# A two-layer attention, SSD and short-convolution kernel: step-size weights as 128 stationary columns, layer 1's rows high and low side by side, and a rule on which PSUM banks the unhurried work may take

## The chip, the cores and the metric

The kernel runs on one core of one Trainium2 chip. The metric is device time in microseconds (us). The kernel before took 1831.9 us, the median of three runs (1830.51 to 1834.58). A core has a matrix engine (PE, whose weight loads the profile lists as PEld), a vector engine (DVE), a scalar engine (ACT), a general engine (POOL) and SyncE (SP), which here issues most DMAs. Matmuls write to PSUM, which has eight banks of 128 partitions by 512 words of 4 bytes.

## The reference

The reference runs two layers over 256 latent tokens and 256 context tokens of width 2048. Layer 0 has neighbourhood attention and a bidirectional state-space scan (SSD), fed by one input projection. Two of its parts matter here. Step sizes, for each of 2 x 32 heads:

```python
dt = jax.nn.softplus(dt_raw + dt_bias)        # dt_raw = 64 columns of h @ w_in, 512 tokens
a = -jnp.exp(a_log)                           # the scan uses cumulated sums of dt * a
```

Layer 1 is a gated short convolution over the 256 latent tokens:

```python
p = h @ w_in                                  # 2048 x 8192
bg, cg, hv, g = jnp.split(p, 4, axis=-1)
y = bg * dw_conv(cg * hv, conv_w)             # 3 taps along the tokens
out = (jax.nn.silu(g) * y) @ w_out            # 2048 x 2048
```

A conditioning vector gives each layer a shift, a scale and a gate: matrix-vector products with `ada_w`, most of them done on DVE.

## The kernel before, in words

**Precision.** Every large product is done in three matmuls on numbers cut in two: a high part H (the value rounded to `fp32r`, a 32-bit type that the matrix engine takes at a faster rate) and a low part Lo (value minus H). A product of weights and rows is H·high + H·low + Lo·high. Each matmul loads its own 128-column stationary operand and streams its moving operand of 256 or 512 columns, one per token or per weight column.

**Weights.** `weight` queues loads of at most 512 KB (128 x 1024 words) from HBM, issued from SP into `raw` buffers. `split` makes H with a cast on ACT (L383) and Lo with a subtraction on DVE (L384). There are three pairs of H and Lo buffers (`NW = 3`), so that the cast for a load begins when the matmuls on the load three places earlier are done. `chunk` runs the matmuls of one load; `use` and `used` open and close it. All matmuls but the transposes have line L188, the helper `mm`; the transposes have L192.

**Order.** The order on every engine is fixed while the program is built. A planner (`Plan`) keeps a modelled clock for each engine. Work other than the matmuls of `chunk` is written as generators that yield what they wait for. After each few matmuls `pump` asks which generators may go on. Three lists hold them: `urgent` (drains of PSUM), `side` (attention heads and SSD groups) and `back` (the matrix-vector products, `gemv_gen`). A generator that wants a bank asks with `nb=1`. `banks(n)` takes n banks for a projection, and if too few are free it makes the drains go on first, wherever the matrix engine stands.

**Step sizes.** The 64 columns of `COL_DT` come in one load of 16 blocks (128 x 16 x 64). For each of 16 blocks of input channels, H·high, H·low and Lo·high go into the first 64 partitions of one bank, 512 tokens wide: 48 matmuls. `dt_gen` then computes softplus on a 64 x 512 layout with four `tmp` buffers, multiplies by `aneg`, and transposes both results in eight transposes.

**Layer 1, input projection.** For i = 0 to 3 and for each of the parts cg, hv, bg and gate, 512 columns of `sc_in` are projected: 8 loads of 2 blocks, and on each block four groups of 128 columns (`mm_ws` with n = 256). The weights are stationary, the 256 tokens move, and two groups share a bank, so that a part takes two banks. `cg_gen`, `hv_gen`, `bg_gen` and `gg_gen` drain them, in that order through `ordered`; `gg_gen` also makes the high and low halves (`y_0` to `y_15`) of the output projection's input. That projection runs four times over 8 loads, with two blocks and two token tiles on each load, 512 columns moving.

Of the kernel before, what the change touches and what calls it, by code (L numbers as in the profile page):

```python
# [8 lines left out]
F32 = mybir.dt.float32  # L9
# [6 lines left out]
KB = 16  # L16
# [125 lines left out]
def kernel(ctx: ExitStack, tc, x, cx, ada_w, ada_b, w_in, w_out, sc_in, sc_out, rpb, small, const,  # L142
                       strict, out):
# [233 lines left out]
    def split():  # L377
        k = pos["split"]
        raw, v = RAW.pop(k)
        nb, n = v.shape[1], v.shape[2]  # L380
        H = WH[k % NW][:, :nb * n].rearrange("p (b c) -> p b c", b=nb)
        Lo = WL[k % NW][:, :nb * n].rearrange("p (b c) -> p b c", b=nb)
        E(S.copy(H, v))  # L383
        E(V.tensor_tensor(out=Lo, in0=v, in1=H.bitcast(F32), op=ALU.subtract))  # L384
        HL[k] = (H, Lo)
        pos["split"] += 1
        give_raw(raw)
        issue()
# [104 lines left out]
    weight(w_in, 0, 16, COL_DT, 64)  # L493
# [117 lines left out]

    def chunk(kb0, kind, ps, first, last, lhs=None):

        H, Lo = use()
        nb = H.shape[1]
        for j in range(nb):
            kb = kb0 + j
            aH, aL = (hH[kb], hL[kb]) if lhs is None else lhs(kb)
            f, l = first and j == 0, last and j == nb - 1
            if kind == "act":  # L620
                mm_act(ps, aH, aL, H[:, j], Lo[:, j], f, l)
            else:
                mm_ws(ps, aH, aL, H[:, j], Lo[:, j], kind, f, l)
        used()
# [395 lines left out]
    aneg = st([128, 1], "aneg")  # L1020

    def dt_gen(ps):
        p64 = slice(0, 64)
        f, b = slice(0, 32), slice(32, 64)
        yield W_("ACT", ps)
        E(S.activation(aneg[p64], P_("alog")[p64], AF.Exp))
        E(V.tensor_scalar(out=aneg[p64], in0=aneg[p64], scalar1=-1.0, scalar2=None, op0=ALU.mult))
        tv, te, ts, ts2 = tmp(), tmp(), tmp(), tmp()
        v, e, s, s2 = tv[p64], te[p64], ts[p64], ts2[p64]
        E(S.activation(v, ps[p64], AF.Identity, bias=P_("dtb")[p64], scale=1.0))  # L1030
        give(free_b, ps)
        E(S.activation(e, v, AF.Abs))
        E(S.activation(e, e, AF.Exp, scale=-1.0))
        yield W_("DVE", te)
        E(V.tensor_scalar(out=s, in0=e, scalar1=2.0, scalar2=None, op0=ALU.add))
        E(V.reciprocal(s, s))  # L1036
        yield W_("DVE", ts)
# [3 lines left out]
        for k in (15, 13, 11, 9, 7, 5, 3):  # L1041
            yield W_("DVE", te)
            E(V.scalar_tensor_tensor(out=e, in0=e, scalar=1.0 / k, in1=s2, op0=ALU.add, op1=ALU.mult))
        yield W_("DVE", te)
        E(V.scalar_tensor_tensor(out=e, in0=e, scalar=1.0, in1=s, op0=ALU.add, op1=ALU.mult))
        E(V.tensor_scalar(out=v, in0=v, scalar1=0.0, scalar2=None, op0=ALU.max))
        E(V.scalar_tensor_tensor(out=v, in0=e, scalar=2.0, in1=v, op0=ALU.mult, op1=ALU.add))
        da = s2
        E(V.tensor_scalar(out=da, in0=v, scalar1=aneg[p64], scalar2=None, op0=ALU.mult))
        give(free_t, te, ts)  # L1050
        hm, ha = half(), half()
        dtm, dam = hm.rearrange("p (t c) -> p t c", t=4), ha.rearrange("p (t c) -> p t c", t=4)
        for src, dst in ((v, hm), (da, ha)):
            yield W_("PE", src, nb=1)
            pt = bank()
            for t in range(4):
                turn(pt[:, t * 64:(t + 1) * 64], src[:, t * 128:(t + 1) * 128])
            yield W_("DVE", pt)
            E(V.tensor_copy(dst, pt[:, :256]))
            give(free_b, pt)  # L1060
        give(free_t, tv, ts2)
# [3 lines left out]
        sS = half()  # L1065
# [35 lines left out]
        rw = tmp()  # L1101
# [295 lines left out]
    H, Lo = use()  # L1397
    for kb in range(KB):
        o = psD[:64, :]
        mm(o, H[:, kb], hH[kb], kb == 0, False)  # L1400
        mm(o, H[:, kb], hL[kb], False, False)
        mm(o, Lo[:, kb], hH[kb], False, kb == KB - 1)
        pump()
    used()
    spawn(urgent, dt_gen(psD), 4, 3)
# [85 lines left out]
    r1 = st([128, 2], "r1")  # L1491
    rb1 = []
# [17 lines left out]
    def norm_gen():  # L1510
# [13 lines left out]
        def low(kb):  # L1524
            E(V.scalar_tensor_tensor(out=hls[kb][:, 1], in0=late[kb], scalar=S1[:, kb:kb + 1], in1=hls[kb][:, 0].bitcast(F32),
                                     op0=ALU.add, op1=ALU.subtract))
            hH[kb], hL[kb] = hls[kb][:, 0], hls[kb][:, 1]
# [58 lines left out]

    def cg_gen(i, ps):
        for b in range(2):
            yield W_("ACT", ps[b])
            E(S.copy(flat(cg, b), ps[b]))  # L1590
            give(free_b, ps[b])

    def hv_gen(i, ps):
        for b in range(2):
            yield W_("DVE", ps[b], flat(cg, b))
            E(V.tensor_tensor(out=flat(u, b), in0=ps[b], in1=flat(cg, b), op=ALU.mult))
            give(free_b, ps[b])
        for b in range(4):
            ch = 4 * i + b
            yield W_("ACT", u[:, b, :])  # L1600
            E(S.mul(v[:, b, :], u[:, b, :], scw[:, 1, ch:ch + 1]))
            yield W_("DVE", v[:, b, :])
# [5 lines left out]
    def bg_gen(i, ps):  # L1608
        for b in range(2):
            yield W_("DVE", ps[b], flat(v, b))  # L1610
            E(V.tensor_tensor(out=flat(v, b), in0=ps[b], in1=flat(v, b), op=ALU.mult))
            give(free_b, ps[b])

    def gg_gen(i, ps):
        for b in range(2):
            yield W_("ACT", ps[b])
            th = tmp()
            E(S.activation(th, ps[b], AF.Tanh, scale=0.5))
            yield W_("DVE", th)
            E(V.scalar_tensor_tensor(out=th, in0=th, scalar=1.0, in1=ps[b], op0=ALU.add, op1=ALU.mult))  # L1620
            give(free_b, ps[b])
            yield W_("DVE", th, flat(v, b))
            E(V.tensor_tensor(out=flat(v, b), in0=flat(v, b), in1=th, op=ALU.mult))
            give(free_t, th)
            for j in range(2):
                kb = 4 * i + 2 * b + j
                yield W_("ACT", v[:, 2 * b + j, :])
                hl = st([128, 2, 256], f"hH{kb}", F32R, name=f"y2_{kb}")
                E(S.copy(hl[:, 0], v[:, 2 * b + j, :]))
                E(V.tensor_tensor(out=hl[:, 1], in0=v[:, 2 * b + j, :], in1=hl[:, 0].bitcast(F32), op=ALU.subtract))  # L1630
                y2[kb] = hl

    for i in range(4):
        for part, gen in ((1, cg_gen), (2, hv_gen), (0, bg_gen), (3, gg_gen)):
            ps = banks(2)
            for kb in range(0, KB, 2):
                force(lambda: hL[kb + 1] is not None)
                chunk(kb, 256, ps, kb == 0, kb == KB - 2)
            spawn(urgent, ordered(4 * i + (1, 2, 0, 3).index(part), gen(i, ps)), 1 if part == 3 else 0)
# [30 lines left out]
_INS = ['x', 'cx', 'ada_w', 'ada_b', 'w_in', 'w_out', 'sc_in', 'sc_out', 'rpb', 'small', 'const', 'strict']  # L1670
# [48 lines left out]
```

## Time and profile before

| what | value |
|---|---|
| median of three runs | 1831.9 us |
| the profiled execution's own time | 1833.06 us |
| its span, first to last instruction | 1831.3 us |
| instructions | 28234 |
| bytes moved by DMA | 376.95 MB, 206 GB/s over the span |
| TensorE clock granted over the span | 0.997 of full |

The span ends 1.8 us short of the execution's own time, which is what lies around the program. The stages in the trace: up to 100 us the loads set the pace; layer 0 with its output projection runs to about 1357 us; a normalisation stands between the layers; layer 1's input projection runs from 1365 to about 1738 us and its output projection to the end.

In the profile a matmul's duration (0.28 us for 256 columns, 0.39 us for 512) is its time from issue to its modelled end. Consecutive matmuls overlap, so what a matmul costs is the distance between two starts, which the view in order of time shows.

### The profile page before, as it was taken

Reading aid. Unit: us, or ns where it says so; the run is one execution under the profiler, and the core shown is the slowest. Engines: PE = TensorE matmul, PEld = TensorE weight load, DVE = VectorE, ACT = ScalarE, POOL = GpSimd, SP = SyncE. Lnnn points to the kernel's source line nnn. Section 1 sums busy time; section 2 is a strip of 40 time slices with the busy share of each in tenths; the row PEclk is TensorE's granted clock in tenths of the full one; section 3 lists DMA queues with packets and bytes.
Section 4 is the critical chain, followed back from the end, with each engine's and each line's share of the span. In section 5 each row is a group of like instructions: output and inputs, shape, how many; then the busy total and the mean of one; then the engine's idle time right before and its main releaser. Section 6 shows DMA issues by size and latency. Waiting matters only on the chain.

```text
span 1831.3 us, 28234 instructions
## 1 busy us (share of the span) xinstructions
PE 1798.7 (98%) x11003; PEld 1546.3 (84%) x11003; DVE 1236.5 (68%) x1943; ACT 762.6 (42%) x1303; POOL 29.5 (2%) x27
## 2 busy tenths in 40 slices
PE   6999999999999999999999999999999999999998
PEld 4677977888888888888878898888879999999987
DVE  5566785877565887575876678756667666555555
ACT  5322533445232445242444345544444344444442
POOL 0000000001000001000001000000000000000000
PEclk9999999999999999999999999999999999999999
DMA  9997644575656575655564557777867777656564
GB/s 327 334 299 250 213 130 122 160 226 175 185 166 190 160 230 179 191 184 187 161 202 144 185 168 221 219 223 261 271 220 230 228 235 239 209 183 181 183 209 155
DMA packets 249062, 376.95 MB, mean 206 GB/s; under 512 B 32624, under 2 KB 103888, under 8 KB 248928
## 3 DMA queue, kind: packets, MB, share of 16 engines
q1 hardware_dynamic: 239632, 366.57, 64.2%
q10 hardware_dynamic: 9296, 8.57, 1.4%
q8 instruction: 86, 1.41, 0.3%
q14 instruction: 48, 0.39, 0.1%
HBM read 368.63 MB, written 7.77 MB: 206 GB/s over the span
## 4 chain that ended last, share of the span: by engine, by line
PE 77%; issue 10%; DVE 4%; DMA 3%; ACT 2%; SPq 0%; POOL 0%; ACTq 0%; POOLq 0%; DVEq 0%
PE bank L188 75%; PE bank L192 2%; DMA tmp<-dram_csr 2%; DVE wL L384 1%; ACT wH L383 1%; DMA raw<-in_w_in 1%; DVE tmp L1122 1%; DVE tmp L1292 0%; DVE tmp L1303 0%; DMA raw<-in_w_out 0%; DVE tmp L1036 0%; ACT tmp L885 0%; DVE acc L752 0%; ACT tmp L1288 0%; DVE tmp L1306 0%
## 5 line engine op out<-in xcount | busy, mean ns | idle before, releaser
L384 DVE TENSOR_TENSOR wL<-raw,wH 128x1024 fp32r<-128x1024 f32 (+1 forms) x440 | 533.9, 1217 | 352.0 <-ACT wH L383 350.7
L383 ACT CAST wH<-raw 128x1024 fp32r<-128x1024 f32 (+1 forms) x440 | 458.9, 1045 | 736.9 <-PE bank L188 648.8
L188 PE MATMUL bank<-h,wH 128*128 128x256 f32 x2048 | 371.5, 284 | 1.3 <-ACT h L1534 1.1
L188 PE MATMUL bank<-hH,wH 128*128 128x256 f32 (+2 forms) x1040 | 352.8, 339 | 0.9 <-ACT wH L383 0.9
L188 PE MATMUL bank<-hL,wH 128*128 128x256 f32 (+2 forms) x1040 | 338.1, 325 | 0.0
L188 PE MATMUL bank<-hH,wL 128*128 128x256 f32 (+2 forms) x1040 | 337.3, 324 | 0.6 <-DVE wL L384 0.5
L188 PEld LDWEIGHTS bank<-h,wH 128*128 128x128 f32 x2048 | 320.9, 193 | 2.7 <-ACT h L1534 1.3
L188 PE MATMUL bank<-h,wL 128*128 128x256 f32 x1024 | 290.6, 284 | 0.0
L188 PE MATMUL bank<-wH,hH 128*128 128x512 f32 x640 | 258.4, 404 | 3.9 <-ACT hH L695 2.6
L188 PE MATMUL bank<-wL,hH 128*128 128x512 f32 x640 | 251.1, 393 | 0.0
L188 PE MATMUL bank<-wH,hL 128*128 128x512 f32 x640 | 250.2, 392 | 0.1
L752 DVE SCALAR_TENSOR_TENSOR acc<-raw,csil,acc 128x512 f32<-128x512 f32 x256 | 191.9, 750 | 71.7 <-DMA raw<-in_ada_w 66.7
L188 PEld LDWEIGHTS bank<-hH,wH 128*128 128x128 f32 (+1 forms) x1040 | 195.7, 188 | 25.3 <-issue 7.3
L188 PEld LDWEIGHTS bank<-hH,wL 128*128 128x128 f32 (+1 forms) x1040 | 196.1, 189 | 19.9 <-DVE wL L384 1.7
L188 PEld LDWEIGHTS bank<-hL,wH 128*128 128x128 f32 (+1 forms) x1040 | 196.0, 188 | 19.9 <-issue 4.3
L188 PEld LDWEIGHTS bank<-h,wL 128*128 128x128 f32 x1024 | 197.3, 193 | 0.1
L188 PE MATMUL bank<-wH,mix 128*128 128x512 f32 x512 | 163.5, 396 | 0.0
L188 PEld LDWEIGHTS bank<-wH,hH 128*128 128x128 f32 x640 | 120.5, 188 | 36.3 <-issue 7.1
L188 PEld LDWEIGHTS bank<-wH,hL 128*128 128x128 f32 x640 | 120.5, 188 | 26.3 <-DVE hL L701 0.6
L188 PEld LDWEIGHTS bank<-wL,hH 128*128 128x128 f32 x640 | 120.8, 189 | 24.1 <-DVE wL L397 0.3
L188 PEld LDWEIGHTS bank<-wH,mix 128*128 128x128 f32 x512 | 96.1, 188 | 21.3 <-issue 1.4
L188 PE MATMUL bank<-wL,mix 128*128 128x512 f32 x256 | 99.8, 390 | 0.0
(233 smaller groups left out, 1613.2 us busy)
## 6 DMA issues: line engine op xcount, KB each, us to landing
raw<-in_w_in SPq DMA_DIRECT2D x211, 512.0 KB
raw<-in_ada_w SPq DMA_DIRECT2D x162, 512.0 KB
raw<-in_sc_in SPq DMA_DIRECT2D x128, 512.0 KB
raw<-in_w_out SPq DMA_DIRECT2D x64, 512.0 KB
raw<-in_sc_out SPq DMA_DIRECT2D x32, 512.0 KB
tmp<-dram_csr SPq DMA_DIRECT2D x32, 256.0 KB
PT<-in_ada_w SPq DMA_DIRECT2D x14, 512.0 KB
xtm<-in_ada_w SPq DMA_DIRECT2D x9, 512.0 KB
```

What stands on the lines that cost most here:

```text
L188: E(T.matmul(o, l, r, start=start, stop=stop, skip_group_check=True))
L192: E(T.transpose(o, i, ident if k == 128 else ident[:k, :k]))
L383: E(S.copy(H, v))
L384: E(V.tensor_tensor(out=Lo, in0=v, in1=H.bitcast(F32), op=ALU.subtract))
L752: E(V.scalar_tensor_tensor(out=acc, in0=v[:, j], scalar=csil[:, 2 * k + j:2 * k + j + 1], in1=acc, op0=ALU.mult, op1=ALU.add))
L1122: E(V.scalar_tensor_tensor(out=do, in0=di, scalar=cwh[:, 32 * k + ch:32 * k + ch + 1], in1=do, op0=ALU.mult, op1=ALU.add))
```

## The change

Three edits.

1. **Step sizes.** The load is cut in two of 8 blocks (128 x 8 x 64). `split` writes H into columns 0 to 63 and Lo into columns 64 to 127 of one stationary block. Two matmuls for each block of input channels (with the high and the low rows moving) fill all 128 partitions of a bank: 32 matmuls. `dt_gen` copies the bank to one `tmp`, turns it in four 128 x 128 transposes, adds the halves, and does softplus on a 128 x 256 layout. Bias and decay now come as rows (`rows`, one DMA broadcast to all partitions).
2. **Layer 1.** The rows' high and low parts already lie side by side in `hls` (128 x 2 x 256). `mm_both` moves them as one operand of 512 columns over H, and then the high 256 alone over Lo. Each group of 128 columns has its own bank, so that a part takes four banks; its high and low sums lie in the two halves and are added by `both` (a copy on ACT, an addition on DVE). The four drains now go by 256 columns in four steps instead of 512 in two.
3. **Banks.** In `may`, work from `back` that asks for a bank is held until the free bank that was left first has been left for 3000 ns by the planner's clock.

```diff
+        if hor < 2000 and nb and sorted(plan.last[b.tensor.name] for b in free_b)[nb - 1] + 3000 > now:
+            return False
...
+        if n == 64:
+            W = WH[k % NW].rearrange("p (b c) -> p b c", b=nb)
+            E(S.copy(W[:, :, :64], v))
+            E(V.tensor_tensor(out=W[:, :, 64:], in0=v, in1=W[:, :, :64].bitcast(F32), op=ALU.subtract))
...
-    weight(w_in, 0, 16, COL_DT, 64)
+    for r0 in (0, 1024):
+        weight(w_in, r0, 8, COL_DT, 64)
...
+    def mm_both(ps, act, H, Lo, first, last):
+        for b, o in enumerate(ps):
+            bb = slice(b * 128, (b + 1) * 128)
+            mm(o, H[:, bb], act, first, False)
+            mm(o[:, :256], Lo[:, bb], act[:, :256], False, last)
+            if b % 2:
+                pump()
...
-        E(S.activation(v, ps[p64], AF.Identity, bias=P_("dtb")[p64], scale=1.0))
...
+        E(DMA.dma_start(rw[:, :128], rows[0].partition_broadcast(128)))
+        yield W_("ACT", ps)
+        E(S.copy(tt, ps))
         give(free_b, ps)
+        yield W_("PE", tt, nb=1)
+        pt = bank()
+        for t in range(4):
+            turn(pt[:, t * 128:(t + 1) * 128], tt[:, t * 128:(t + 1) * 128])
...
-    for kb in range(KB):
-        o = psD[:64, :]
-        mm(o, H[:, kb], hH[kb], kb == 0, False)
-        mm(o, H[:, kb], hL[kb], False, False)
-        mm(o, Lo[:, kb], hH[kb], False, kb == KB - 1)
...
+        for kb in range(8 * k, 8 * k + 8):
+            mm(psD, W[:, kb - 8 * k], hH[kb], kb == 0, False)
+            mm(psD, W[:, kb - 8 * k], hL[kb], False, kb == KB - 1)
...
+    def both(p, o=None):
+        yield W_("ACT", p)
+        o = half() if o is None else o
+        E(S.copy(o, p[:, 256:]))
+        yield W_("DVE", o)
+        E(V.tensor_tensor(out=o, in0=p[:, :256], in1=o, op=ALU.add))
+        give(free_b, p)
+        return o
...
     def gg_gen(i, ps):
-        for b in range(2):
...
+        for b in range(4):
+            kb = 4 * i + b
+            gg = yield from both(ps[b])
+            yield W_("ACT", gg)
+            th = half()
+            E(S.activation(th, gg, AF.Tanh, scale=0.5))
+            yield W_("DVE", v[:, b, :])
+            E(V.tensor_tensor(out=v[:, b, :], in0=gg, in1=v[:, b, :], op=ALU.mult))
...
-            ps = banks(2)
+            ps = banks(4)
...
-                chunk(kb, 256, ps, kb == 0, kb == KB - 2)
+                chunk(kb, "both", ps, kb == 0, kb == KB - 2, lambda i: (h1[i], None))
```

How the order moves on the matrix engine in layer 1: here it begins with the second group of the first block before. `h_0` is the rows' first block with its high and low halves, `wH` and `wL` the cut weights; "x2" is the matmul with the high and then with the low half.

```order
L188 MATMUL bank_86<-h_0_10398,wH_99 128x256 x2
L188 MATMUL bank_86<-h_0_10398,wL_102 128x256
L188 MATMUL bank_90<-h_0_10398,wH_99 128x256 x2
L188 MATMUL bank_90<-h_0_10398,wL_102 128x256
L188 MATMUL bank_90<-h_0_10398,wH_99 128x256 x2
L188 MATMUL bank_90<-h_0_10398,wL_102 128x256
```

The same place after the change:

```order
L188 MATMUL bank_85<-h_0_10352,wL_100 128x256
L188 MATMUL bank_90<-h_0_10352,wH_97 128x512
L188 MATMUL bank_90<-h_0_10352,wL_100 128x256
L188 MATMUL bank_89<-h_0_10352,wH_97 128x512
L188 MATMUL bank_89<-h_0_10352,wL_100 128x256
L188 MATMUL bank_84<-h_0_10352,wH_97 128x512
L188 MATMUL bank_84<-h_0_10352,wL_100 128x256
```

Three matmuls of 256 columns on one group became one of 512 and one of 256, and four banks are written in turn instead of two.

The second place is DVE at the seam between layer 1's two projections, before the change. `wL` rows are the weight subtractions of `split`; `y_12` to `y_15` are the last four blocks of the output projection's input, written here by `gg_gen` for i = 3. The first subtraction shown belongs to the output projection's load 3, counted from 0, and the second to load 4.

```order
L384 TENSOR_TENSOR wL_101<-raw_93,wH_98 128x1024
L1630 TENSOR_TENSOR y_12_14149<-v,y_12_14149 128x256
L1630 TENSOR_TENSOR y_13_14152<-v,y_13_14152 128x256
L1620 SCALAR_TENSOR_TENSOR tmp_66<-tmp_66,bank_91 128x512
L1623 TENSOR_TENSOR v<-v,tmp_66 128x512
L384 TENSOR_TENSOR wL_102<-raw_94,wH_99 128x1024
L1630 TENSOR_TENSOR y_14_14182<-v,y_14_14182 128x256
L1630 TENSOR_TENSOR y_15_14185<-v,y_15_14185 128x256
```

After the change, the end of the same drain, with the subtractions of loads 7, 8 and 9:

```order
L396 TENSOR_TENSOR wL_100<-raw_93,wH_97 128x1024
L1668 TENSOR_TENSOR y_14_13332<-v,y_14_13332 128x256
L1622 TENSOR_TENSOR half_77<-bank_87,half_77 128x256
L396 TENSOR_TENSOR wL_101<-raw_94,wH_98 128x1024
L1661 TENSOR_TENSOR v<-half_77,v 128x256
L1663 SCALAR_TENSOR_TENSOR v<-half_83,v 128x256
L396 TENSOR_TENSOR wL_102<-raw_95,wH_99 128x1024
L1668 TENSOR_TENSOR y_15_13370<-v,y_15_13370 128x256
```

`y_15` moved from behind the subtraction of load 4 to behind that of load 9; between two of the four blocks there are now two weight subtractions.

The third place is the matrix engine in the step-size product. Before, three rows for one block of input channels:

```order
L188 MATMUL bank_91<-hH_328,wH_98 64x512
L188 MATMUL bank_91<-hL_332,wH_98 64x512
L188 MATMUL bank_91<-hH_328,wL_101 64x512
L192 MATMUL bank_87<-const,tmp_66 128x128 x4
L188 MATMUL bank_91<-hH_519,wH_98 64x512
```

After it, two rows for a block:

```order
L188 MATMUL bank_90<-hH_321,wH_98 128x512
L188 MATMUL bank_90<-hL_325,wH_98 128x512
L192 MATMUL bank_87<-const,tmp_66 128x128 x4
L188 MATMUL bank_90<-hH_328,wH_98 128x512
L188 MATMUL bank_90<-hL_332,wH_98 128x512
```

The matmul with the separate `wL` is gone, and the other two write 128 partitions instead of 64; the transposes between them are another generator's.

More of the change, by code (lines that the diff above doesn't have):

```diff
@@ L142 @@
 def kernel(ctx: ExitStack, tc, x, cx, ada_w, ada_b, w_in, w_out, sc_in, sc_out, rpb, small, const,
-                       strict, out):
+                       strict, rows, out):
     nc = tc.nc
@@ L1491 @@
     r1 = st([128, 2], "r1")
+    h1 = {}
     rb1 = []
@@ L1585, in ordered @@
         seq[0] += 1
+    def both(p, o=None):
[6 more added lines that the diff above has]
+        return o
     def cg_gen(i, ps):
-        for b in range(2):
-            yield W_("ACT", ps[b])
-            E(S.copy(flat(cg, b), ps[b]))
-            give(free_b, ps[b])
+        for b in range(4):
+            yield from both(ps[b], cg[:, b, :])
     def hv_gen(i, ps):
[L1594 to L1597, printed above, removed]
         for b in range(4):
             ch = 4 * i + b
+            yield from both(ps[b], u[:, b, :])
+            yield W_("DVE", u[:, b, :])
+            E(V.tensor_tensor(out=u[:, b, :], in0=u[:, b, :], in1=cg[:, b, :], op=ALU.mult))
             yield W_("ACT", u[:, b, :])
             E(S.mul(v[:, b, :], u[:, b, :], scw[:, 1, ch:ch + 1]))
+        for b in range(4):
+            ch = 4 * i + b
             yield W_("DVE", v[:, b, :])
@@ L1608, in bg_gen @@
     def bg_gen(i, ps):
[L1609 to L1612, printed above, removed]
-    def gg_gen(i, ps):
[L1615 to L1618, printed above, removed]
-            yield W_("DVE", th)
[L1620 to L1631, printed above, removed]
+        for b in range(4):
+            bg = yield from both(ps[b])
+            yield W_("DVE", bg, v[:, b, :])
+            E(V.tensor_tensor(out=v[:, b, :], in0=bg, in1=v[:, b, :], op=ALU.mult))
+            give(free_h, bg)
@@ new lines, in gg_gen @@
+    def gg_gen(i, ps):
+        for b in range(4):
+            kb = 4 * i + b
[5 more added lines that the diff above has]
+            E(V.tensor_tensor(out=v[:, b, :], in0=gg, in1=v[:, b, :], op=ALU.mult))
+            yield W_("DVE", th)
+            E(V.scalar_tensor_tensor(out=v[:, b, :], in0=th, scalar=1.0, in1=v[:, b, :], op0=ALU.add, op1=ALU.mult))
+            give(free_h, gg, th)
+            yield W_("ACT", v[:, b, :])
+            hl = st([128, 2, 256], f"hH{kb}", F32R, name=f"y2_{kb}")
+            E(S.copy(hl[:, 0], v[:, b, :]))
+            E(V.tensor_tensor(out=hl[:, 1], in0=v[:, b, :], in1=hl[:, 0].bitcast(F32), op=ALU.subtract))
+            y2[kb] = hl
@@ L1667 @@
     force(lambda: not urgent, (urgent,))
-_INS = ['x', 'cx', 'ada_w', 'ada_b', 'w_in', 'w_out', 'sc_in', 'sc_out', 'rpb', 'small', 'const', 'strict']
+_INS = ['x', 'cx', 'ada_w', 'ada_b', 'w_in', 'w_out', 'sc_in', 'sc_out', 'rpb', 'small', 'const', 'strict', 'rows']
 def kernel(**inputs):
@@ L1706 @@
         'w_out': f('na_ssd_w_out')[0], 'sc_in': f('sc_w_in')[0], 'sc_out': f('sc_w_out')[0], 'rpb': f('na_rpb')[0],
-        'small': small, 'const': const, 'strict': strict}
+        'small': small, 'const': const, 'strict': strict,
+        'rows': np.concatenate([f('ssd_dt_bias')[0].reshape(1, 64), f('ssd_a_log')[0].reshape(1, 64)], axis=1)}
     nc = bacc.Bacc("TRN2", target_bir_lowering=False, num_devices=1)
```

77 lines of the change are left out of this document (42 added, 35 removed).

## The prediction

> **What bounds the kernel now.** The first part of the page, the busy time of each engine, comes first.
>
> ```profile
> PE 1798.7 (98%) x11003; PEld 1546.3 (84%) x11003; DVE 1236.5 (68%) x1943; ACT 762.6 (42%) x1303; POOL 29.5 (2%) x27
> ```
>
> The matrix engine is busy all the time, with DVE at two thirds. That share is a mean, so the next view is the busy time by stage (stretch, its length, then PE, PEld, DVE, ACT and POOL with counts, the granted clock, DMA share, GB/s).
>
> ```profile
> 100.00:1350.00 1250.00, 1247.82 (x6905) 1039.67 (x6904) 889.35 (x1463) 517.52 (x976) 25.88 (x16) 1.00 0.64 197
> 1350.00:1400.00 50.00, 46.16 (x324) 43.27 (x323) 35.84 (x60) 27.42 (x45) 0.70 (x1) 0.93 0.58 192
> ...
> 1737.00:1831.00 94.00, 88.77 (x395) 73.04 (x393) 51.66 (x55) 33.87 (x36) 0.00 (x0) 1.00 0.58 182
> ```
>
> Layer 0 leaves PE idle for 2.2 of 1250 us, the seam between the layers for 3.8. Then the chain that ended last, in order of time: start, length, what.
>
> ```profile
> 1364.99 19.62 PE bank L188 x144
> 1384.62 1.21 DVE wL L384
> 1385.83 0.33 DVE yi L1532
> 1386.16 0.41 DVE h L1525
> ```
> ```profile
> 1386.61 438.50 PE bank L188 x3320
> ```
>
> From 1386.6 us to 1825 us the chain is one row of matmuls: no wait stands in it. In layer 1 a matmul's start-to-start distance is time itself, so I read those distances from the view in order of time (start, length, instruction).
>
> ```profile
> 1499.87 0.28 PE L188 MATMUL bank<-h,wL 128*128 128x256 f32 x1
> ...
> 1501.67 0.28 PE L188 MATMUL bank<-h,wL 128*128 128x256 f32 x1
> ```
> ```profile
> 195.69 0.39 PE L188 MATMUL bank<-wH,hL 128*128 128x512 f32 x1
> ...
> 200.00 0.39 PE L188 MATMUL bank<-wL,hH 128*128 128x512 f32 x1
> ```
>
> Between the first two rows lie five rounds of three matmuls: 15 in 1.80 us, 120.0 ns for 256 columns. Between the other two lie 19 steps in 4.31 us: 226.8 ns for 512. Twice the columns do not cost twice the time. A line through both has 0.417 ns for a column and 13.2 ns for a matmul whatever its length. On that 13.2 ns the forecast rests.
>
> **Layer 1's input projection.** It has 16 parts x 16 blocks x 4 groups = 1024 groups. Before, a group takes three matmuls of 256: 360.0 ns. After, it takes one of 512 and one of 256: 346.8 ns. The columns streamed stay 768; one matmul with its weight load goes. 1024 x 13.2 ns = **13.5 us**, all on the path, since nothing else ends there.
>
> The trace has no stream that alternates 512 and 256, so the pair has to be bounded. On the good side, the weight loads fill the all-256 stream:
>
> ```profile
> 1500.00:1550.00 50.00, 50.00 (x419) 50.00 (x418) 33.97 (x41) 19.42 (x21) 0.00 (x0) 1.00 0.73 239
> ```
>
> PEld is busy 50.00 of 50 us there. If loads are what holds 256 columns at 120 ns, a 256 beside a 512 could come down to half of 226.8, which is 113.4: a pair of 340 and a gain of 20.3 us. On the bad side, the longest distance for 512 columns that repeats is in the step-size product:
>
> ```profile
> 231.15 0.40 PE L188 MATMUL bank<-hH,wH 128*64 128x512 f32 x1
> ...
> 235.78 0.40 PE L188 MATMUL bank<-hH,wL 128*64 128x512 f32 x1
> ```
>
> 20 steps in 4.63 us: 231.5 ns. With that and a 256 as much worse (124), the pair is 355 and the gain 5 us. I take 346.8, because the two rows it is made of are long streams of just these operations, and because 64 stationary columns cost no less than 128: the surcharge goes with the instruction, not with the load's width.
>
> The Trainium skill speaks against this gain. "TensorE: Matmul & The Clock Gate", section "Back-to-back issue gap", gives N/2.4 + 2.5 ns between matmuls. That would be 109 and 216 ns, a fixed part of 2.5 ns, and here a gain of 1024 x 2.5 = 2.6 us (an estimate from that page). The trace agrees on the slope (0.417) and not on the fixed part (13.2).
>
> **What the drains add.** Each bank now costs a copy on ACT and an addition on DVE, and the products run by 256. The nearest rows, by group (count, then busy us and mean ns, idle before):
>
> ```profile
> L384 DVE TENSOR_TENSOR wL<-raw,wH 128x1024 fp32r<-128x1024 f32 x121 | 147.6, 1224 | 125.2 <-ACT wH L383 125.2
> L383 ACT CAST wH<-raw 128x1024 fp32r<-128x1024 f32 x120 | 125.7, 1047 | 192.9 <-PE bank L188 183.0 <-DVE acc L742 3.8 <-issue 1.5
> ...
> L1596 DVE TENSOR_TENSOR u<-bank,cg 128x512 f32<-128x512 f32 x8 | 5.1, 682 | 0.0
> ...
> L1590 ACT COPY cg<-bank 128x512 f32<-128x512 f32 x8 | 4.3, 586 | 0.0
> L1623 DVE TENSOR_TENSOR v<-v,tmp 128x512 f32<-128x512 f32 x6 | 4.2, 692 | 0.2
> ```
> ```profile
> 1390.00:1737.00 347.00, 347.00 (x2904) 346.00 (x2904) 210.75 (x238) 142.99 (x162) 0.00 (x0) 1.00 0.68 213
> ```
> ```profile
> 291.05 0.42 DVE L1011 TENSOR_TENSOR half<-bank,gt 128x256 f32<-128x256 f32 x1 [0.57 <-PE bank L188]
> ```
>
> For each i, eight DVE operations at 0.69 us (5.5 us) become 32 at 0.42 (13.4 us), and four on ACT at 0.59 become 16 copies and four tanh at about 0.4 (2.4 to 8 us). Over the window that is some 30 us more on DVE (to about 72% busy) and 20 on ACT (to about 49%). Both had been idle waiting for the matrix engine's progress (125 and 183 us, the releasers above), so I cost it at nothing. If that cover were gone, the price is the slower rival below.
>
> The banks: all eight are now used, four filling and four draining. The order shows the gate's drain as four steps with two weight subtractions in each. A load lasts 8 x 346.8 ns = 2.77 us, so that a step is about 5.6 us and the last bank comes free about 3 x 5.6 + 2 = 19 us into the next part, which takes 22.2 us. So nothing waits there.
>
> At the seam to the output projection something does. `y_15` now stands on DVE behind the weight subtraction of load 9, whose cast begins only when load 6 is done; and load 7 is what needs `y_15`.
>
> ```profile
> 1749.36 1.05 ACT L383 CAST wH<-raw 128x1024 fp32r<-128x1024 f32 x1 [1.69 <-PE bank L188]
> ```
> ```profile
> 1742.16 1.23 DVE L384 TENSOR_TENSOR wL<-raw,wH 128x1024 fp32r<-128x1024 f32 x1 [0.32 <-ACT wH L383]
> 1743.30 0.75 DVE L1630 TENSOR_TENSOR y<-v,y 128x256 fp32r<-128x256 f32 x2
> ...
> 1750.43 1.22 DVE L384 TENSOR_TENSOR wL<-raw,wH 128x1024 fp32r<-128x1024 f32 x1 [1.51 <-ACT wH L383]
> ```
>
> After load 6: cast to subtraction 1.07, subtraction to `y` 1.14, `y` 0.4, together 2.7 us. The matrix engine has 8 matmuls before it needs that low part, 1.8 us. **Cost 0.9 us.**
>
> At the start of layer 1 the chain quoted above shows the first part held by the normalisation at 1384.62 (wL, then yi, then h). The order is the same there after the change, so a faster matrix engine partly waits: of its first part's 64 x 13.2 ns = 0.85 us I give back 0.5.
>
> **Step sizes.** 48 matmuls become 32, all 512 columns long; a 64-column stationary block costs 231.5 ns, no less than a full one: 16 x 231.5 = **3.7 us**. The transposes go from eight of 64 columns to four of 128, which cancels. Two loads of half the size move the same 256-byte pieces past the same SP queue; they need two `raw` buffers and two weight slots for a while. The chain behind it gets shorter:
>
> ```profile
> 244.82 3.35 DVE L1036 RECIPROCAL tmp<-tmp 64x512 f32<-64x512 f32 x1
> ```
>
> At half the width this should be near 1.7 us, and the steps behind it shrink likewise. Layer 0's matrix engine hardly idles, so I count nothing for it. The `strict` load now waits on SP for the decay product; its generator asks for it only when the planner has that product done, so that the weight loads behind it are not held for long.
>
> **The bank rule.** It concerns the matrix-vector products alone.
>
> ```profile
> L188 PE MATMUL bank<-acc,const 128*32 128x128 f32 x24 | 1.3, 285 | 0.0
> ```
>
> Nothing waited before them (idle 0.0), so there is nothing to save before; it guards the fuller banks after. Its result can come later: the order has 12 of the 16 products ahead of layer 1 now, not 13, and the last well before the output projection. Cost nothing.
>
> **Reordering.** The edit at 230 us shifts what is interleaved in all of layer 0. By PE's idle time there is only 2.2 us to win; stalls shorter than a matmul's modelled length do not show, so I allow 4 us either way, middle zero.
>
> **Sum.** 1833.06 - 13.5 - 3.7 + 0.9 + 0.5 = 1817.3 us in the terms of the profiled execution. The median of the runs stands 1.2 us below that execution, so the forecast is **1816.1 us**, 0.9% faster.
>
> **Rivals.**
> *Loads were the limit* (the 340 ns pair): 6.8 us more, 1809.3. For it speaks PEld at 50.00 of 50; against it, that 512 columns, where loads have twice the time, carry the same surcharge. Chance 0.09.
> *The surcharge does not go with the instruction.* If a short matmul between long ones pays for the one that was dropped, a group stays at 360 ns and only the step sizes are left: 1816.1 + 13.5 = 1829.6. Nothing in the trace has this mix, so it cannot be excluded; the straight line is against it. Chance 0.05.
> *Most of it goes with the group.* If only about 2.5 of the 13.2 ns belong to a matmul and the rest is paid once for a group of 128 columns, layer 1 gains 2.6 us: 1827.0. The straight line is against this too, since the 512-column stream changes its group as often as the other and pays the same. Chance 0.03. The rule of the Trainium skill above ("TensorE: Matmul & The Clock Gate") amounts to this.
> *The drains hold the banks*, which ends slower. Let s be a step of the gate's drain. A part begins late by 3s + 2 - 22.2 us, three times; the seam by about 4s - 20.9 (at s = 5.45, eight loads of the output projection's 2.72 us in four steps, that is the 0.9 above). At s = 5.6 the first is nothing; at s = 7.9 both together are 21 us, which eats the gain and 3.7 us more, and that is the point from which it decides. With a third weight subtraction in each step (s = 8.4) they come to 15 + 12.7 = 27.7 us, 26.8 over the forecast: 1842.9. Against it, DVE has 28% of the stage free. Chance 0.05.
> *The change does not do what it says*: the order shows the 512 and 256 pairs and the 32 matmuls, so this is left only for the bank rule, at no price.
>
> **How the numbers follow.** The forecast has 0.78, with its own range of 1811 to 1823: the 4 us of reordering, and the pair within about 2 ns. The range for 8 in 10 goes down to 1808 for the first rival and up to 1824.5 for the pair at 355 ns. A measurement can tell 0.2%, 3.7 us, from no change: faster 0.90 (the forecast, the loads and the group), the same 0.05, slower 0.05.
>
> **What would show it.** In order of time, starts in layer 1 should go 227, 120, 227, 120 ns; a sum of 340 or 360 names the rival. The step-size product should last about 7.4 us instead of 11. The output projection's load 7 should begin with a wait of 1 us on DVE `y`, and no other row but PE should stand in the chain from 1390 us on. DVE or ACT drains in the chain in layer 1, or a wait at the first matmul of a part, would be the slower rival. A layer 0 that ends more than 4 us off (its output projection now ends at 1357 us, and 3.7 us earlier is expected) would make the prediction wrong for a reason not worked out here.

## The result, and the profile after

| | before | after |
|---|---|---|
| median of six runs each | 1832.62 us (1830.51 to 1834.58) | 1822.1 us (1820.64 to 1825.36) |
| ratio, 95% interval | | 0.994 (0.993 to 0.9951) |
| the profiled execution's own time | 1833.06 us | 1820.64 us |
| its span | 1831.3 us | 1818.9 us |

The change is faster by 10.5 us, 0.6%; 15.8 us (0.9%) had been forecast. The forecast of 1816.1 us lies 6.0 us under the median, and its range holds it. The profiled execution of the changed kernel is the fastest of its six, so that the two traces stand 12.4 us apart, and it is those 12.4 us that the views can place.

The page's first part, the busy time of each engine, of the changed kernel:

```profile
PE 1785.2 (98%) x9959; PEld 1488.2 (82%) x9959; DVE 1259.2 (69%) x2039; ACT 777.4 (43%) x1369; POOL 28.5 (2%) x27
```

There are 1044 matmuls fewer, and the share of PE is still 98%: the program got shorter with its bound, and the bound is the same. DVE and ACT did more (1236.5 and 762.6 us before), in less time. The busy time by stage of the changed kernel (columns as in the prediction):

```profile
100.00:1350.00 1250.00, 1248.66 (x6895) 1043.44 (x6894) 877.71 (x1450) 518.99 (x978) 24.90 (x16) 1.00 0.64 195
1350.00:1400.00 50.00, 45.08 (x243) 37.93 (x243) 36.83 (x63) 27.22 (x46) 0.70 (x1) 0.97 0.58 188
1400.00:1720.00 320.00, 320.00 (x1850) 277.41 (x1849) 233.48 (x327) 149.80 (x210) 0.00 (x0) 1.00 0.73 228
1720.00:1819.00 99.00, 92.72 (x410) 75.52 (x408) 55.15 (x64) 36.14 (x43) 0.00 (x0) 0.99 0.57 180
```

From 1400 to 1720 us PE is busy 320.00 of 320 us: no wait for a drain shows (one shorter than the overlap of two matmuls would not). DVE is at 73% there (233.48 of 320) and ACT at 47%. PEld, which was full before (50.00 of 50), is at 87%. The chain that ended last in the changed kernel (start, length, what):

```profile
1381.66 360.68 PE bank L188 x2055
1742.33 1.35 issue
1743.68 1.06 ACT wH L395
1745.10 0.81 issue
1746.38 66.37 PE bank L188 x289
```

Before, one row of matmuls ran from 1386.61 to 1825 us. Now it breaks once, at 1742 to 1746 us, where a cast on ACT stands in it: the seam to the output projection.

Each stage's length, from the first matmul of one stage to that of the next, in the views in order of time of both kernels (us). For the changed kernel the first two of these matmuls are:

```profile
1360.56 0.79 PE L188 MATMUL bank<-h,wH 128*128 128x512 f32 x1 [1.57 <-DVE h L1553]
...
1724.27 0.39 PE L188 MATMUL bank<-wH,y 128*128 128x512 f32 x1
```

| stage | before | after | change | forecast |
|---|---|---|---|---|
| up to layer 1's first matmul | 1364.99 | 1360.56 | -4.4 | -3.7 |
| layer 1's input projection | 373.13 | 363.71 | -9.4 | -13.0 |
| output projection, to its last matmul | 87.26 | 88.76 | +1.5 | +0.9 |
| behind it, to the end | 5.88 | 5.82 | -0.1 | 0 |
| sum | | | -12.4 | -15.8 |

One of the 16 matrix-vector products moved over the border of the first two rows: 12 run ahead of layer 1 and four in it, where there were 13 and three. A part of layer 1 with such a product is 0.54 us longer than one without. Without that shift the first row is -3.9 and the second -9.9. The first row is less sure than it looks: nine of the ten kernels of the experiments below keep the changed kernel's order on the matrix engine up to there, and over these nine traces and its own, layer 1's first matmul starts anywhere between 1358.62 and 1363.07 us.

So the miss is nearly all in layer 1's pairs. The changed kernel's matmuls there, in order of time (start, length), in two stretches 50 us apart:

```profile
1449.85 0.40 PE L188 MATMUL bank<-h,wH 128*128 128x512 f32 x1
1450.08 0.28 PE L188 MATMUL bank<-h,wL 128*128 128x256 f32 x1
...
1451.93 0.40 PE L188 MATMUL bank<-h,wH 128*128 128x512 f32 x1
...
1499.69 0.40 PE L188 MATMUL bank<-h,wH 128*128 128x512 f32 x1
1499.92 0.28 PE L188 MATMUL bank<-h,wL 128*128 128x256 f32 x1
...
1501.81 0.40 PE L188 MATMUL bank<-h,wH 128*128 128x512 f32 x1
```

Six pairs take 2.08 us in the first and 2.12 us in the second: 346.7 ns a pair, which is the forecast to a tenth, and 353.3 ns. Followed through the stage, the stream is in one or the other of these two states for tens of microseconds: 346.7 from 1365 to 1374 us, 353.3 to 1415 (with the first part's waits for its weights at 1376 to 1382 us), 346.7 to 1496, 353.3 to 1578, 346.7 to 1662, 353.3 to the end. The mean behind the first part, without the products, is 350.1. At each change from 1415 us on stands a matrix-vector product, as at the second of them:

```profile
1495.61 0.40 PE L188 MATMUL bank<-h,wH 128*128 128x512 f32 x1
1495.84 0.28 PE L188 MATMUL bank<-h,wL 128*128 128x256 f32 x1
1496.05 0.43 PE L188 MATMUL bank<-acc,const 128*32 128x128 f32 x8
1496.40 0.50 PE L188 MATMUL bank<-h,wH 128*128 128x512 f32 x1
```

What makes the two states, and what the seam's 1.5 us are, the experiments had to say. The theories to begin with: the drains hold something back (against the forecast); a 512 that alternates with a 256 pays more than in a stream of its own (A); a matmul that goes to another bank than the one before it pays (B). Later came: an odd break in the rhythm flips the state (C); the state lasts until something breaks the stream (D).

### The profile page after: what moved, and what is told of

Its sections match the earlier page's. It is cut to its first block, busy times and chain, and to the rows that moved or that the text cites. A ratio compares the mean times of both kernels' runs of the same rounds, so it can differ in the third digit from the quotient of the medians.

```text
span 1818.9 us, 26339 instructions
## 1 busy us (share of the span) xinstructions
PE 1785.2 (98%) x9959; PEld 1488.2 (82%) x9959; DVE 1259.2 (69%) x2039; ACT 777.4 (43%) x1369; POOL 28.5 (2%) x27
## 4 chain that ended last, share of the span: by engine, by line
PE 84%; issue 8%; DVE 2%; DMA 1%; ACT 1%; POOLq 0%; POOL 0%; SPq 0%; ACTq 0%; DVEq 0%
PE bank L188 82%; PE bank L192 2%; DVE wL L396 1%; DMA raw<-in_ada_w 1%; DMA tmp<-dram_csr 1%; ACT wH L395 0%; DVE tmp L1150 0%; DVE acc L776 0%; DVE h L1553 0%; DVE tmp L1331 0%; DVE hL L725 0%; DVE tmp L1691 0%; DVE tmp L721 0%; DVE tmp L1689 0%; DVE tmp L1334 0%
## 5 line engine op out<-in xcount | busy, mean ns | idle before, releaser
L188 PE MATMUL bank<-h,wH 128*128 128x512 f32 x1024 | 360.9, 398 | 2.0 <-DVE h L1553 2.0
L188 PE MATMUL bank<-hH,wH 128*128 128x256 f32 (+1 forms) x1040 | 353.4, 340 | 0.8 <-ACT wH L395 0.8
L188 PE MATMUL bank<-hL,wH 128*128 128x256 f32 (+1 forms) x1040 | 338.6, 326 | 0.0
L188 PE MATMUL bank<-hH,wL 128*128 128x256 f32 (+1 forms) x1024 | 331.7, 324 | 0.3 <-DVE wL L396 0.3
L188 PE MATMUL bank<-h,wL 128*128 128x256 f32 x1024 | 286.4, 280 | 0.4 <-DVE wL L396 0.4
L188 PEld LDWEIGHTS bank<-h,wH 128*128 128x128 f32 x1024 | 193.0, 188 | 49.6 <-DVE h L1553 2.5
L188 PEld LDWEIGHTS bank<-hH,wH 128*128 128x128 f32 x1040 | 196.8, 189 | 24.3 <-issue 7.4
L188 PEld LDWEIGHTS bank<-hL,wH 128*128 128x128 f32 x1040 | 197.1, 190 | 19.7 <-issue 4.8
L188 PEld LDWEIGHTS bank<-hH,wL 128*128 128x128 f32 x1024 | 194.2, 190 | 18.0 <-DVE wL L396 1.0
L188 PEld LDWEIGHTS bank<-h,wL 128*128 128x128 f32 x1024 | 193.5, 189 | 0.7 <-DVE wL L396 0.7
```

The costliest lines, as they stand in the source:

```text
L188: E(T.matmul(o, l, r, start=start, stop=stop, skip_group_check=True))
```

## The experiments

Each edit is against the changed kernel, where nothing else is said. The kernel before ran on each chip beside them (medians 1832.34 to 1833.82 us), so that between chips the ratios compare; a single run has none.

**Three matmuls in the new banks.** The banks, the drains and the rule stay, and the 512 goes as two of 256:

```diff
-            mm(o, H[:, bb], act, first, False)
+            mm(o[:, :256], H[:, bb], act[:, :256], first, False)
+            mm(o[:, 256:], H[:, bb], act[:, 256:], False, last)
             mm(o[:, :256], Lo[:, bb], act[:, :256], False, last)
```

> The changed kernel with its four banks, drains and bank rule, but each group again in three matmuls of 256 columns. Theory (the gain of layer 1 is the dropped matmul, the drains cost nothing): starts 120 ns apart, and from the first matmul of layer 1 to the first of the output projection about 373 us as before the change (it was 373.1; 363.7 after the change). Rival (fuller banks and longer drains cost time of their own): over 374.5 us, with waits on DVE or ACT rows in the chain.

1828.97 us in one run, beside 1832.74 before. Layer 1 takes 373.89 us, 0.8 more than before, and 0.54 of that is the fourth product; the starts are 120 ns apart as they were. So the drains and the eight banks cost some 0.2 us in this trace, and what layer 1 gains is the matmul that was dropped.

**The block's 512s first, then its 256s**, so that the lengths hardly alternate and every matmul goes to another bank than the one before:

```diff
         for b, o in enumerate(ps):
-            bb = slice(b * 128, (b + 1) * 128)
-            mm(o, H[:, bb], act, first, False)
-            mm(o[:, :256], Lo[:, bb], act[:, :256], False, last)
+            mm(o, H[:, b * 128:(b + 1) * 128], act, first, False)
             if b % 2:
                 pump()
+        for b, o in enumerate(ps):
+            mm(o[:, :256], Lo[:, b * 128:(b + 1) * 128], act[:, :256], False, last)
+        pump()
```

> The changed kernel with the matmuls of a block in another order: the four of 512 columns first, then the four of 256. In the changed kernel a pair costs about 350 ns (234 + 116) where 346.8 was forecast. Theory A (the 3 ns come from alternating long and short matmuls): a block of four groups goes from 1401 to 1387 ns, layer 1's input projection from 363.7 to about 360 us. Theory B (they come from changing the bank with each pair): twice as many changes of bank, so 363.7 us or more, up to 367. The mean of either is within 0.3% of the time, so the trace's starts decide.

1821.81 us, ratio 0.9941 (0.9926 to 0.9956); layer 1 365.13 us, 350.8 ns a pair from start to end, in one state. A is out: hardly a length alternates, and nothing is won. The time lies where B had it.

**512, 256, 256, 512 ...**, which halves the alternations and leaves the bank changes:

```diff
+            if b % 2 == 0 or first:
                 mm(o, H[:, bb], act, first, False)
                 mm(o[:, :256], Lo[:, bb], act[:, :256], False, last)
+            else:
+                mm(o[:, :256], Lo[:, bb], act[:, :256], False, False)
+                mm(o, H[:, bb], act, False, last)
```

> The changed kernel with every second group's two matmuls swapped (512, 256, 256, 512, 512, 256, 256, 512), so that half of the changes between long and short are gone and each pair keeps its bank. Theory A (alternating costs the 3 ns): a block of four groups at about 1394 ns, layer 1's input projection at 362.0 us. Theory B (the bank's change costs them): no difference, 363.7 us.

1819.37 us in one run; layer 1 362.49 us. Four pairs of this kernel in order of time:

```profile
1500.35 0.40 PE L188 MATMUL bank<-h,wH 128*128 128x512 f32 x1
1500.58 0.40 PE L188 MATMUL bank<-h,wL 128*128 128x256 f32 x2
1500.81 0.63 PE L188 MATMUL bank<-h,wH 128*128 128x512 f32 x2
1501.28 0.39 PE L188 MATMUL bank<-h,wL 128*128 128x256 f32 x2
1501.51 0.63 PE L188 MATMUL bank<-h,wH 128*128 128x512 f32 x2
```

Two pairs between the second and the fourth row take 0.70 us. A pair costs 348.3 ns, in the same single state behind each of the products; only around a part's first block, which is not swapped, is it up to 353.3. A block of four pairs is 1393 ns, where A had 1394, and the stage lies between the two forecasts. B as it was put is out: the banks change as often as after. But A, which this run suits, had failed in the blocked order. Nor is it a fixed price for each change of length and each change of bank, both together: the changed kernel, where its pairs are at 346.7 ns, changes length eight times in a block and takes 1387 ns, and the snake changes it four times, with as many changes of bank, and takes 1393. What the order does to the pair is measured; why is open.

**The step sizes alone**: the kernel before with the weights' part of the change, and without the rows of layer 1 and the bank rule.

> The kernel before with the step-size edit alone (no layer 1 edit, no bank rule). Theory: 3.7 us, 1829 us, layer 1 begins at 1361.3 us of the span instead of 1365.0. Rival (what moves in layer 0 decides): layer 1 begins outside 1359 to 1363, and the edit's worth is not that of its matmuls.

1828.71 us (median of ten), ratio 0.9981 (0.9971 to 0.999): 4.0 us. The interval is 1.8 to 5.3 us. Layer 1 begins at 1359.23 us, just inside the 1359 to 1363 that were given, and it and the output projection take 373.68 and 87.26 us, which is before again with its fourth product.

**One short matmul more at the start of each part**, to break the rhythm by one instruction where no product does:

```diff
+            for _ in range(1 if first and b == 0 else 0):
+                mm(o[:, :64], H[:, bb], act[:, :64], True, False)
```

> The changed kernel with one short matmul more (64 columns, overwritten at once) at the start of each of layer 1's 16 parts. In the changed kernel a pair costs either 346.7 or 353.3 ns, and changes from one to the other exactly at the four matrix-vector products of layer 1. Theory C (an odd number of matmuls and loads between turns the state over): the state changes at each part, every 22 us, and once more at each matrix-vector product; the mean stays near 350. Theory D (only a stop of the stream, with its change to another kind of matmul, sets the state anew): it changes at the matrix-vector products alone.

1825.59 us in one run; layer 1 366.43. The state does change at some of these places, and at others it doesn't: it stays at 346.7 from 1457 to 1545 us, over three starts and a product, and at 353.3 from 1581 us to the end, over six starts and a product. C had every one of them flip it, and D as put here, that it changes at the products alone, fails too.

**Two short matmuls** at the same places (`range(2 ...)`), which by C would change nothing:

> The same with two short matmuls at the start of each part. Theory C: an even number turns nothing, so the state changes only at the matrix-vector products. Theory D: the same. If it changes at each part here as well, a short matmul of any number disturbs the state, and C falls.

1821.8 us in one run; layer 1 366.0. Here too the state changes at some starts (1454, 1476, 1544 us) and not at others (1408, 1431). C falls: an odd break and an even one do the same, they may set the state anew. Of D is left that the state lasts until some break.

**The bank rule left out**:

```diff
-        if hor < 2000 and nb and sorted(plan.last[b.tensor.name] for b in free_b)[nb - 1] + 3000 > now:
-            return False
```

> The changed kernel without the rule on banks. Its order is that of the changed kernel up to layer 1; there three of the four matrix-vector products come one to four loads earlier. Theory (the rule costs and saves nothing): within 2 us of the changed kernel, no wait of PE on a bank. Rival (without it such a product takes a bank that a drain still reads): a wait on DVE or ACT ahead of the matmuls of these products, 1 us or more each, 1825 us or more.

1826.02 us, ratio 0.9959 (0.9943 to 0.9975), some 4 us behind the changed kernel in the medians, though the two intervals overlap; layer 1 takes 369.54 us, 5.8 more than the changed kernel's, and up to it the order is the same. The matrix engine in order of time, where the product of this kernel comes:

```profile
1409.88 0.28 PE L188 MATMUL bank<-h,wL 128*128 128x256 f32 x1
1412.07 0.43 PE L188 MATMUL bank<-acc,const 128*32 128x128 f32 x8 [1.92 <-DVE u L1620]
...
1413.22 0.63 PE L188 MATMUL bank<-h,wH 128*128 128x512 f32 x1
...
1413.87 0.63 PE L188 MATMUL bank<-h,wH 128*128 128x512 f32 x1
```

and the stretches behind it (granted clock third from the end):

```profile
1412.00:1415.80 3.80, 3.73 (x19) 3.05 (x20) 1.99 (x6) 1.53 (x4) 0.00 (x0) 0.56 0.48 147
1415.80:1420.00 4.20, 4.20 (x25) 3.63 (x25) 2.56 (x4) 1.90 (x2) 0.00 (x0) 0.99 0.09 17
```

The product was given a bank that a drain on DVE had yet to read (the addition of `u` at 1411.60 us), and the matrix engine stood for 1.92 us, with the projection's matmuls, which need nothing from that bank, behind the product in the order. Then it ran at a granted clock of 0.56 over 3.8 us (by single microseconds from 1412 us on 0.74, 0.50, 0.50, 0.56 and then 1.00): the pair between 1413.22 and 1413.87 us takes 0.65 us. A second product, at 1573.57 us, waits 0.58 us, and no slow stretch follows. The part with the first wait is 26.69 us long, where a part with a product and every pair at 353.3 ns is 23.16; the part with the second is 23.77. So the waits cost 3.5 and 0.6 us, and that is what the rule saves; the other 1.7 us of layer 1 are more pairs at 353.3 ns.

**The seam.** The last drain of the gate goes as two sequences, blocks 0 and 2 and blocks 1 and 3, so that `y_15` is ready a load earlier:

```diff
-    def gg_gen(i, ps):
-        for b in range(4):
+    def gg_gen(i, ps, bs=(0, 1, 2, 3)):
+        for b in bs:
...
+            if part == 3 and i == 3:
+                for bs in ((0, 2), (1, 3)):
+                    spawn(urgent, ordered(15, gg_gen(i, ps, bs)), 0, 2)
+                continue
```

> The changed kernel with the last gate drain (i = 3) as two generators side by side, blocks 0 and 2 and blocks 1 and 3, so that y_15 stands on DVE behind the weight subtraction of load 6 and not of load 9. Theory: the wait at the output projection's load 7 goes, the output projection takes 87.3 us as before the change instead of 88.8, and the time falls by 1.5 us. Rival (the wait is hidden by something later): the output projection stays at 88.8 us.

1819.75 us, ratio 0.9925 (0.9913 to 0.9938), which overlaps the changed kernel's interval; the output projection takes 87.26 us again, as before the change, and it is this stage that shows the gain. The profiled execution itself (1820.67 us) is no shorter than the changed kernel's, because its layer 1 began 1.5 us later. The chain of this kernel ends with one row of matmuls:

```profile
1379.78 432.99 PE bank L188 x2377
```

**The seam and the snake order together**:

> The changed kernel with the swapped matmuls in every second group and the last gate drain as two generators. In the swapped order a pair cost 348.3 ns over the whole of layer 1, without two states. Theory: layer 1's input projection 362.5 us, the output projection 87.3 us, 1.3 us below the kernel with the gate drain alone and near 1818.5 us, faster than the kernel before and after the change. Rival (the swapped order's 348.3 was the chance of one run): pairs of 346.7 or 353.3 again, and no more than 1 us from the kernel with the gate drain alone.

1817.33 us (1816.65 to 1820.54), ratio 0.9922 (0.9908 to 0.9936): 15.0 us under the kernel before, and the lowest median of all. Layer 1 takes 362.33 us and the output projection 87.27. Its pairs are at 348.3 ns in one state again, so that was not the chance of one run. By layer 1 in the traces of the two experiments (363.74 and 362.33 us) the snake order is worth 1.4 us beside the seam alone; the two ratios cannot tell that.

**No product in layer 1**: the four last products' matmuls are left out, and a copy stands in for their result, so that layer 1's gate is missing from the output:

```diff
+            if n >= 12:
+                yield W_("DVE", acc)
+                E(V.tensor_copy(rowb, acc[:, :128]))
+            else:
...
```

> The changed kernel without the matmuls of the four matrix-vector products that fall into layer 1 (a copy stands in their place, so that layer 1's gate is left out of the result as it should be). Theory D (the state of the pairs lasts until the stream of matmuls is broken): after the first part one state from end to end, all pairs at 346.7 or all at 353.3; the input projection 2.5 us shorter than the changed kernel's for the missing products (0.57 us each) and another 3.4 us shorter or longer by the state. Rival (the state turns over with time): it changes within the stage, about every 80 us, all the same.

1823.59 us in one run; layer 1 364.63 us. Apart from the first part's waits for its weights all pairs are 353.3 ns, and no state changes. By stretches of 70 us without a product, first of this kernel, then of the changed one:

```profile
1420.00:1490.00 70.00, 70.00 (x398) 60.71 (x397) 55.05 (x79) 32.61 (x49) 0.00 (x0) 1.00 0.74 247
1500.00:1570.00 70.00, 70.00 (x399) 60.67 (x398) 56.27 (x83) 33.95 (x50) 0.00 (x0) 1.00 0.75 243
```
```profile
1420.00:1490.00 70.00, 70.00 (x406) 61.23 (x405) 55.35 (x79) 32.89 (x47) 0.00 (x0) 1.00 0.75 241
1500.00:1570.00 70.00, 70.00 (x399) 60.74 (x397) 57.40 (x85) 34.28 (x53) 0.00 (x0) 1.00 0.75 237
```

PE issues 398 and 399 matmuls in both stretches here, 406 and then 399 in the changed kernel, with the same granted clock and about the same traffic. What is left of D holds in this: without a break the state stays for 343 us (1384 to 1727), so here it isn't time, the parts or the drains that change it. In the kernels with short matmuls, and in the one without the bank rule, some breaks change it and some don't. It is not chance from run to run alone: the kernel with the seam split has the changed kernel's order of all 9959 matmuls, and its trace has the same states between the same products. Why a break leaves the one state or the other is open.

## Why the prediction was right, and where its size was off

**What bounds the kernel**: right. The matrix engine's starts set the time in layer 1, and each matmul that went was worth its fixed part on the path.

**Layer 1's input projection**: the mechanism was right, and the term was mis-sized. The step was: "I take 346.8, because the two rows it is made of are long streams of just these operations". Both rows were true, and the pair does cost their sum, in one of two states (226.7 + 120.0 ns); in the other, which holds for half of the stage, it costs 6.6 ns more. The mean is 350.1. Over the 960 pairs behind the first part that is 9.9 ns each, 9.5 us, where 13.2 ns had been taken: 3.2 us of the miss. The row for 512 columns came from a stream with the rows stationary, and 226.8 ns is only one of the speeds at which the trace has 512 columns. The prediction took 231.5 ns, on 64 stationary columns, for the longest distance for 512 columns that repeats, and used it for the bound only. That reading was wrong: the kernel before has streams of 512 columns over 128 columns of stationary weights, the pair's own form, that go at two speeds. One of them, in order of time:

```profile
549.64 0.39 PE L188 MATMUL bank<-hH,wL 128*128 128x512 f32 x1
...
570.74 0.39 PE L188 MATMUL bank<-hH,wL 128*128 128x512 f32 x1
571.42 0.39 PE L188 MATMUL bank<-hH,wL 128*128 128x512 f32 x1
...
589.78 0.39 PE L188 MATMUL bank<-hH,wL 128*128 128x512 f32 x1
```

90 steps in 21.10 us are 234.4 ns, then 81 steps in 18.36 us 226.7, at a granted clock of 1.00 in both and with no other matmul in between; streams from 823 and from 1021 us do the same. With 234.4 the pair comes to 354.4, with 226.7 to 346.7, near the two states that were measured, and half way between to 350.6. So the size could have been read off the trace before. That the pair's states are these two speeds is likely by the sums, and not shown. The 13.2 ns are no constant of an instruction: they depend on the order of the stream, 346.7 to 353.3 ns for the pair with the same two instructions in it (348.3 in the snake, 350.8 in blocks of four).

The formula of the Trainium skill, "TensorE: Matmul & The Clock Gate", section "Back-to-back issue gap", gave an estimate of 2.6 us for the stage. The trace disagrees: 9.9 ns went with each matmul, not 2.5. The section calls this formula the gap of an isolated matmul, apart from a stream in which each matmul brings its weight load, so it spoke less against the gain than the prediction had it.

**The first part of layer 1**: 25.91 us before, 25.44 after, so 0.4 of the 0.85 us are given back; 0.5 had been taken.

**The drains**: right, no price. The groups of the changed kernel between 1390 and 1724 us (count, busy us, mean ns, idle before):

```profile
L396 DVE TENSOR_TENSOR wL<-raw,wH 128x1024 fp32r<-128x1024 f32 x119 | 145.3, 1224 | 85.1 <-ACT wH L395 83.7
...
L1622 DVE TENSOR_TENSOR half<-bank,half 128x256 f32<-128x256 f32 x28 | 11.7, 418 | 0.0
L1620 ACT COPY half<-bank 128x256 f32<-128x256 f32 x28 | 9.1, 374 | 0.0
```

The additions cost the 0.42 us that had been read off layer 0, and the subtraction ahead of them still idles 85.1 us, 83.7 of them for ACT. The slower rival, the drains that hold the banks, did not come; the kernel with three matmuls puts their price at some 0.2 us.

**The seam**: right in place, short in size: 1.5 us for 0.9. The matrix engine of the changed kernel, in order of time, and then ACT and DVE there:

```profile
1744.57 1.01 PE L188 MATMUL bank<-wH,y 128*128 128x512 f32 x2
1745.42 0.40 PE L188 MATMUL bank<-wL,y 128*128 128x512 f32 x1
1746.38 0.74 PE L188 MATMUL bank<-wH,y 128*128 128x512 f32 x2 [0.56 <-DVE y L1668]
```
```profile
1743.68 1.05 ACT L395 CAST wH<-raw 128x1024 fp32r<-128x1024 f32 x1 [1.35 <-issue]
1744.64 0.40 ACT L1667 CAST y<-v 128x256 fp32r<-128x256 f32 x1
```
```profile
1744.77 1.22 DVE L396 TENSOR_TENSOR wL<-raw,wH 128x1024 fp32r<-128x1024 f32 x1 [0.63 <-ACT wH L395]
1745.91 0.42 DVE L1668 TENSOR_TENSOR y<-v,y 128x256 fp32r<-128x256 f32 x1
```

The forecast followed the low part of `y_15`: cast, subtraction, `y`, and that path is there (1743.68, 1744.77, 1745.91, then PE at 1746.38). It left out that the high part stands on ACT behind the same cast, to 1745.04, and holds the matrix engine first: the pair of matmuls at 1744.57 lasts 1.01 us. Load 7 takes 3.99 us in place of 2.72, which is 1.3; the four loads behind it take 2.80 in place of 2.75 us, the other 0.2: 12 matmuls of 512 columns at 233.3 ns in place of 229.2, so a stream of one length too goes at more than one speed behind a wait. The kernel with the seam split has all of the 1.5 us back.

**The step sizes**: right. In order of time in the changed kernel:

```profile
227.49 0.48 PE L188 MATMUL bank<-hH,wH 128*128 128x512 f32 x1
...
235.21 0.39 PE L188 MATMUL bank<-hL,wH 128*128 128x512 f32 x1
235.44 0.28 PE L188 MATMUL bank<-hH,wH 128*128 128x256 f32 x1
```

From the first row to the last are 7.95 us. One group of transposes of other work lies between (0.36 us), and the matmul behind it and the first row, which follows another group, take 0.09 us more each: 7.4 us, as the prediction had it. In the same way it was 11.1 before. That is 3.7 us, the forecast; by itself the edit gave 4.0 us in the medians. Layer 0's new order shows no cost beside the 4.5 us by which layer 1's start differs between traces of one order.

**The bank rule**: "no price" was right beside the kernel before, which had no such wait. What the change would be without it the prediction left out ("it guards the fuller banks after"): 4.1 us of waits and half clock, by the experiment's trace. It is not an ornament of the change but a part of its gain.

**From the trace to the median**: the sum missed by 3.4 us in the terms of the traces (3.2 the pairs, 0.6 the seam, -0.4 the rest). The other 2.6 us are not in any term: 1.2 us had been taken off because the kernel before ran that much under its profiled execution, while the changed one's median stands 1.5 us above its own. The other five executions have no trace. More pairs at 353.3 ns in layer 1 are not the likely cause, since the seam experiment, with the same order of matmuls, took 363.74 us there against 363.71. More likely is the time up to layer 1: it differs by 4.5 us between ten traces of the same order, the spans of the six executions by 4.7, and the profiled one, at 1360.56 us, lies 0.6 us under the mean of the ten. So the 6.0 us between forecast and median are 3.4 us of sizes and 2.6 us that lie within what executions differ by.

## What to carry to other kernels

Where the matrix engine is never idle, count instructions before columns: fewer, longer matmuls won 9.9 ns for each one dropped, and the price was the banks and the drains, which cost nothing as long as the drains' engines have slack and nobody is handed a bank that a drain has yet to read. Take the cost of a matmul from a stream in its own form and order, look through the whole trace for a second speed of that form, and where two rows differ by 2%, carry both into the sum. At a seam, follow each operand of the first late matmul, the high half and the low, along the queue of its own engine.

## What the runs showed of the hardware

- A steady stream of the same two matmuls has two speeds, 346.7 and 353.3 ns a pair, at a granted clock of 1.00. In layer 1 it keeps one for as long as nothing breaks it (343 us in one kernel), and a few short matmuls in between may change it. A stream of 512 columns alone has two as well, 234.4 and 226.7 ns, and in layer 0 of the kernel before it went from one to the other without a break. The same pairs in another order have one speed alone: 348.3 ns (512, 256, 256, 512) or 350.8 (four 512s, four 256s).
- A wait of 1.92 us on the matrix engine was followed by 3.8 us at a granted clock of 0.56, of which some 3.4 us at half (an estimate from the single microseconds above); one of 0.58 us was not. The Trainium skill, "TensorE: Matmul & The Clock Gate", section "Part 1: The HAM clock gate", has the clock halve after an idle window of about 3.4 us. Here less than that was enough, and the measurement decides; that it is back to full after about 3.4 us of work, as the page has it, agrees with the trace.
